# Layer 0's normalisation moved to the values' PSUM bank, and its and the convolution's elementwise instructions given places in the written order

## The chip, the cores and the metric

The kernel runs on one core of one Trainium2 chip. The metric is the device time of one execution in microseconds; the time of a kernel is the median of its runs. The core's engines are TensorE (PE, with its weight loads shown as PEld), VectorE (DVE), ScalarE (ACT), GpSimd (POOL) and SyncE (SP, which issues the DMAs). Each engine takes its instructions in the order of its own queue.

## The reference, cut to what matters

The reference is a two-layer diffusion backbone in fp32 over 2048 tokens plus 256 context tokens, 1024 channels. Each layer normalises, projects, mixes in two branches, projects out and adds. The change lies in the mixer of layer 0:

```python
def even_mixer(px, pc, lam_p, subln, conv_w, lam_init, row, col, need_ctx):
    ...
    o = lax.map(lambda qb: diff_attend(qb, k_all, v_all, lam), q_blocks)
    ...
    out_a = diff_attention_post(o, subln, lam_init).astype(px.dtype) * jax.nn.silu(ga)
    out_b = short_conv(bb, cb, ub, conv_w) * jax.nn.silu(gb)
```

`diff_attend` takes two softmaxes over 2304 keys for each of 8 heads and subtracts one, times lambda, from the other, before the product with the values. `diff_attention_post` is an RMS norm over the 64 channels of a head. `short_conv` multiplies two projections, c and u, runs a three-tap convolution along the tokens, and multiplies by a third projection, b.

## The kernel before, in words

Layer 0's attention is `attention0`. It works on pairs of 128-query tiles: 64 periods j, each with two tiles n, for 8 heads of 16 tiles. For a tile, with m one of the two softmaxes: QK writes scores of 768 keys into one of two PSUM buffers "ps" (each two banks, L981); TR, one VectorE instruction, copies the scores out and takes their minimum (`reduce_scores`, L758); EX is the exponential over 2304 keys on ScalarE (L1020); CF, CD, PS and PA combine the two softmaxes, the first CD=192 columns on VectorE (L1034) and the rest in two halves of 1056 columns on GpSimd (L1039, L1044); T transposes on TensorE (L1051), E copies the result out on ScalarE (L1058); AV is the product with the values (L1068) into "po", a pool with a single bank; MA and MD add the two halves of po into the tile "ob" (L1079, L1089).

The order is written out by hand in `ATT_ORDER`: a list of operations with a planned time in ns each. An operation of period j stands at its time plus j times `ATT_PERIOD` (17966). The operations of all periods are sorted by that time and issued in that order; the planned times set only the order. `pin` chains an instruction to the pinned one before it on the same engine, so that pinned instructions keep that order. Instructions that aren't pinned are placed in their queue by the framework's scheduler.

The convolution's three projections fill TensorE: `conv_units` yields 2592 matmuls in 108 groups of 24 (L704), all into one PSUM bank "y0". The ten F of a period issue 4.18 matmuls each (`FILL`), and an F stops at the end of a group. At a group's end elementwise instructions follow, none of them pinned: after the first projection ScalarE copies the bank out (L719), after the second VectorE multiplies it (L721), after the third come three taps (POOL L728, DVE L729, L730), the gate (DVE L735) and the last product (POOL L739).

At the end of every fourth tile pair of an odd head MD starts `normalise` for the tile ob of 512 tokens: `squares` on ScalarE (L769), `means` with four small products "pms" (L775) and six small VectorE and GpSimd instructions on "f" and "zf" (L779 to L784), `rows` with four transposing products "pf" (L789) and a copy "fr" (L792), `scale` with a product "pr" (L796; each of the nine shows as two matmuls), a load of the gate "ga" (L798) and two VectorE instructions (L799, L800). The four steps are issued 1000, 2500, 8000 and 13000 ns of planned time after MD. Only their matmuls are pinned. The three products take the scores' buffers: `fin` is a `_Bank` over the pool of ps. There are 16 normalisations, every other period of the odd heads.

When the convolution is done, F loads the output weights (`load_wout`; 16 splits on POOL and DVE, L1171 and L1172), the gate rows and the first output product, in steps put into a list "late" at planned times. They end before `out_ctx`, which begins at the last QK.

Of the kernel before, what the change touches and what calls it, by code (L numbers as in the profile page):

```python
# [9 lines left out]
F32 = mybir.dt.float32  # L10
F32R = mybir.dt.float32r
AF = mybir.ActivationFunctionType
# [32 lines left out]
LX0:6277 QK011:6323 EX00:7115 TR011:7204 QK012:7706 F2:8053 TR012:8243 QK100:8753 F3:9100 TR100:9290 F4:9582  # L45
QK101:10064 LS01:10326 EX01:10530 TR101:10601 QK102:10847 F5:11194 F6:11676 TR102:12056 QK110:12158 F7:12941
LS10:13142 RC0:13296 F8:13423 CF0:13504 QK111:13905 LX1:14124 EX10:14374 CD0:14683 PS00:14988 TR110:14988
TR111:16024 PA00:16266 QK112:16703 TR112:17240 F9:17486 PS01:18785 LS11:18875 EX11:19108 PA01:20063 T00:21324
RC1:21701 T01:21760 CF1:21909 E00:21960 CD1:22582 PS10:22887 E01:23652 T02:23854 PA10:24165 E02:24490
T03:24637 T04:26502 PS11:26684 E03:27492 PA11:27963 E04:28084 T10:28378 T11:30472 E10:30907 E11:31499  # L50
AV0:32314 AV1:33174 T12:34234 E12:34870 T13:35017 E13:35653 T14:36282 E14:36700 AV2:36942 AV3:37802 AV4:38662
MA:41240 MD:47571
# [58 lines left out]


class _Bank(_Tags):


    width = None

    def tile(self, shape, dtype, tag, **kw):
        x = super().tile([shape[0], self.width or shape[1]], dtype, tag, **kw)
        return x[:, :shape[1]]  # L120
# [32 lines left out]
class Backbone:  # L153
# [488 lines left out]
    def conv_units(self, es):  # L642

        nc = self.nc
# [43 lines left out]
        for si, (j, ci) in enumerate(steps):  # L688
# [4 lines left out]
            for br in range(3):  # L693
# [17 lines left out]
                zc = z[:, 2:2 + n]  # L711
                if br == 0:
                    if first:
                        nc.gpsimd.memset(z[:, 0:2], 0.0)
                    else:
                        nc.gpsimd.tensor_copy(z[:, 0:2], ez)
                    if last:
                        nc.gpsimd.memset(z[:, n + 2:n + 3], 0.0)
                    nc.scalar.activation(zc, ps, AF.Copy)  # L719
                elif br == 1:  # L720
                    nc.vector.tensor_tensor(zc, ps, zc, ALU.mult)  # L721
                else:
# [5 lines left out]
                    nc.gpsimd.tensor_scalar(yc, z[:, i0 + 1:i1 + 1], wc[1], None, ALU.mult)  # L728
                    nc.vector.scalar_tensor_tensor(yc, z[:, i0:i1], wc[0], yc, ALU.mult, ALU.add)  # L729
                    nc.vector.scalar_tensor_tensor(yc, z[:, i0 + 2:i1 + 2], wc[2], yc, ALU.mult, ALU.add)  # L730
                    g = cp.tile([P, n + 1], F32, tag="g", name="cg")
                    nc.sync.dma_start(g[:, 1:1 + n], self.gb[j * P:j * P + P, t0:t0 + n])
                    if not first:
                        nc.vector.tensor_copy(g[:, 0:1], eg)
                    nc.vector.tensor_tensor(g[:, 1:1 + n], ps, g[:, 1:1 + n], ALU.mult)  # L735
                    if not last:
                        nc.gpsimd.tensor_copy(ez, z[:, n:n + 2])
                        nc.vector.tensor_copy(eg, g[:, n:n + 1])
                    nc.gpsimd.tensor_tensor(yc, yc, g[:, i0:i1], ALU.mult)  # L739
                    rows = slice(j * P, j * P + P)  # L740
                    cols = slice(t0 - 1 + i0, t0 - 1 + i1)
                    nc.sync.dma_start(self.mixb[0][rows, cols], yc)

                yield False
# [16 lines left out]
    def normalise(self, ep, pp, hp, o, zi, t0, n, tags=("sq", "fr", "sq"), bank="fin"):  # L761
# [3 lines left out]
        f = ep.tile([P, 8], F32, tag="f", name="f")[:, :2 * nt]  # L765

        def squares():
            self.sq = ep.tile([P, n], F32, tag=tags[0], name="sq")
            nc.scalar.activation(self.sq, o, AF.Square)  # L769

        def means():
            sq = self.sq
            pms = pp.tile([P, 512], F32, tag=bank, name="pms")
            for j in range(nt):
                self.pin(nc.tensor.matmul(pms[:, 2 * j:2 * j + 2], sq[:, j * P:j * P + P], self.blk,  # L775
                                          start=True, stop=True))

            zf = ep.tile([P, 8], F32, tag="zf", name="zf")[:, :2 * nt]
            nc.vector.tensor_copy(zf, zi.rearrange("p t h m -> p (t h) m")[:, :, 0])  # L779
            nc.vector.tensor_tensor(f, pms[:, :2 * nt], zf, ALU.mult)  # L780
            nc.vector.tensor_tensor(f, f, zf, ALU.mult)
            nc.vector.tensor_scalar(f, f, EPS, None, ALU.add)
            nc.gpsimd.tensor_tensor(f, f, self.mhalf.to_broadcast([P, 2 * nt]), ALU.pow)
            nc.vector.tensor_tensor(f, f, zf, ALU.mult)  # L784

        def rows():
            pf = pp.tile([P, 512], F32, tag=bank, name="pf")
# [102 lines left out]
    def attention0(self, ws, xs, ys, ps_t, ps_o):  # L890
# [1088 lines left out]
```

## Time and profile before

| | us |
|---|---|
| median of 3 runs | 3417.8 (3413.26 to 3419.44) |
| the profiled execution, its own time | 3412.76 |
| span of the profiled execution | 3411.0 |
| PE busy | 3224.7 |
| DVE busy | 1818.6 |
| ACT busy | 1604.1 |
| POOL busy | 1460.4 |

The span is the time from the first instruction to the last; the execution's own time lies 1.8 us above it. Busy times are over the whole span, and the stages differ: projections before and after the attention keep PE alone busy, while in the attention of layer 0 four engines work side by side.

### The profile page before, as it was taken

What the parts mean: (1) busy time and instruction counts of PE and PEld (TensorE: products, weight loads), DVE (VectorE), ACT (ScalarE), POOL (GpSimd) and SP (SyncE); (2) the same over time, 40 slices, a digit from 0 to 9 for tenths busy, and PEclk for the clock granted to TensorE, in tenths of its full rate; (3) what the DMA queues carried; (4) which work ended last, traced back from release to release, by engine and by line L of the source; (5) the groups of instructions that cost most, each with busy time, mean ns of one, the idle gap of its engine ahead of it and who ended that gap; (6) DMA issues with size and microseconds to landing.
All of it is one profiled execution on the core that took longest, in us unless ns stands there. A gap on an engine that the chain in (4) does not pass through costs nothing.

```text
span 3411.0 us, 54003 instructions
## 1 busy us (share of the span) xinstructions
PE 3224.7 (95%) x20386; PEld 2611.9 (77%) x20386; DVE 1818.6 (53%) x4155; ACT 1604.1 (47%) x2521; POOL 1460.4 (43%) x1185
## 2 busy tenths in 40 slices
PE   7999999999899988998899889999999999989999
PEld 6877777777677766776777657898888887878887
DVE  4343322477787787778777765421121014656733
ACT  4311133477777776776677634331111123656401
POOL 3133200388678867886778754300021001433400
PEclk9999999999999999999999989999999999999999
DMA  7366643623242334242323225443223157954143
GB/s 251 127 209 219 209 124 105 192 77 123 87 128 97 104 106 124 82 131 93 116 72 120 76 68 167 173 152 111 96 93 105 68 159 197 227 147 133 51 148 117
DMA packets 305317, 442.08 MB, mean 130 GB/s; under 512 B 54837, under 2 KB 212001, under 8 KB 292258
## 3 DMA queue, kind: packets, MB, share of 16 engines
q1 hardware_dynamic: 305058, 438.64, 40.4%
q8 instruction: 161, 2.64, 0.3%
q14 instruction: 98, 0.80, 0.1%
HBM read 307.59 MB, written 131.43 MB: 129 GB/s over the span
## 4 chain that ended last, share of the span: by engine, by line
PE 77%; DVE 10%; issue 6%; ACT 2%; POOL 2%; DMA 2%; SPq 0%; DVEq 0%; POOLq 0%; ACTq 0%
PE mm L394 27%; PE cmm L704 7%; PE po L1068 7%; PE y L1196 6%; PE pt L1051 6%; PE ps L981 6%; PE mm L406 4%; DVE s L758 4%; PE po L1894 3%; PE ps L1843 3%; PE pt L1877 3%; PE mps L307 1%; PE pc L1684 1%; ACT s L1020 1%; DVE f L784 1%
## 5 line engine op out<-in xcount | busy, mean ns | idle before, releaser
L758 DVE CUSTOM_DVE_ANT_0 s<-ps,zero 128x768 f32<-128x768 f32 x768 | 721.0, 953 | 215.6 <-PE ps L981 205.0
L394 PE MATMUL mm<-hx,wh 128*128 128x512 f32 (+1 forms) x2784 | 830.9, 382 | 0.0
L1044 POOL TENSOR_TENSOR s<-s 128x1056 f32<-128x1056 f32 x256 | 628.3, 2454 | 16.9
L394 PEld LDWEIGHTS mm<-hx,wh 128*128 128x128 f32 x2784 | 505.6, 188 | 122.5 <-issue 18.0
L394 PE MATMUL mm<-hx,wl 128*128 128x512 f32 (+1 forms) x1392 | 528.5, 380 | 0.0
L1058 ACT ACTIVATE aT<-pt 128x512 f32<-128x512 f32 (+1 forms) x640 | 345.4, 552 | 247.6 <-PE pt L1051 245.4
L981 PE MATMUL ps<-kst,qst 128*128 128x512 f32 (+1 forms) x1536 | 427.6, 367 | 36.1 <-DVE mx L758 34.1
L704 PE MATMUL cmm<-cx,wh 128*128 128x256 f32 x1728 | 353.7, 291 | 71.2 <-ACT z L719 25.3
L1039 POOL TENSOR_SCALAR s<-s,cf 128x1056 f32<-128x1056 f32 x256 | 314.2, 1227 | 240.1 <-DVE cf L1029 62.9
L1051 PE MATMUL pt<-sm,s 128*128 128x128 f32 x2304 | 357.0, 278 | 1.4 <-ACT aT L1058 1.1
L704 PEld LDWEIGHTS cmm<-cx,wh 128*128 128x128 f32 x1728 | 274.9, 191 | 93.5 <-ACT z L719 30.1
L1051 PEld LDWEIGHTS pt<-sm,s 128*128 128x128 f32 x2304 | 267.7, 142 | 70.6 <-issue 50.9
L1020 ACT ACTIVATE s<-s,bias 128x2304 f32<-128x2304 f32 x128 | 283.7, 2217 | 45.7 <-DVE bias L1009 45.2
L394 PEld LDWEIGHTS mm<-hx,wl 128*128 128x128 f32 x1392 | 261.3, 188 | 53.4
L1068 PE MATMUL po<-aT,vt 128*64 128x256 f32 x2304 | 290.8, 396 | 0.0
L1020 ACT ACTIVATE s<-s,low 128x2304 f32<-128x2304 f32 x128 | 283.6, 2216 | 5.1
L981 PEld LDWEIGHTS ps<-kst,qst 128*128 128x128 f32 x1536 | 236.1, 192 | 65.2 <-DVE mx L758 54.1
L704 PE MATMUL cmm<-cx,wl 128*128 128x256 f32 x864 | 247.6, 287 | 0.0
L1068 PEld LDWEIGHTS po<-aT,vt 128*64 128x64 f32 x2304 | 157.0, 140 | 99.8 <-issue 37.8
L1855 POOL TENSOR_SCALAR s<-s,rz 128x832 f32<-128x832 f32 (+1 forms) x128 | 122.8, 959 | 201.2 <-DVE rz L1854 150.9
L1196 PE MATMUL y<-wh,mh 128*128 128x512 f32 x544 | 182.4, 414 | 1.6 <-DVE mh L1274 1.6
L1196 PE MATMUL y<-wh,mx 128*128 128x512 f32 x544 | 174.4, 399 | 0.5 <-DVE mx L1276 0.5
(266 smaller groups left out, 4687.5 us busy)
## 6 DMA issues: line engine op xcount, KB each, us to landing
cx<-hx SPq DMA_DIRECT2D x72, 1024.0 KB
hx<-hx SPq DMA_DIRECT2D x18, 1024.0 KB
kst<-k SPq DMA_DIRECT2D x192, 96.0 KB
k<-k SPq DMA_DIRECT2D x32, 576.0 KB
xt<-in_x_dram SPq DMA_DIRECT2D x32, 512.0 KB
wm<-in_w_mod_dram SPq DMA_DIRECT2D x64, 256.0 KB
qst<-q SPq DMA_DIRECT2D x256, 64.0 KB
ws<-in_w_in_even_dram SPq DMA_DIRECT2D x27, 512.0 KB
```

Source lines behind the costliest of these rows:

```text
L394: mm = self.nc.tensor.matmul(ps[:, :n], p[:, kc], y, start=first, stop=last)
L406: mm = self.nc.tensor.matmul(ps[:, :3 * P], q[kc][:, ts] if isinstance(q, list) else q[:, kc, ts], p[:, kc], start=first, stop=last)
L704: yield nc.tensor.matmul(ps, w[p][:, kc, :], x[q][:, kc, :], start=i == 0, stop=i == 23)
L758: return self.nc.vector.tensor_tensor_reduce(dst, ps, self.zero.to_broadcast([P, n]), -QS, BIGGEST, ALU.add, ALU.min, mx)
L981: pin(nc.tensor.matmul(ps[:, k0:k1], q[:, qc:qc + P], k[:, k0:k1], start=True, stop=True))
L1020: pin(nc.scalar.activation(it.s[m], it.s[m], AF.Exp, bias=bias, scale=-1.0, accum_out=it.Z[:, m:m + 1]))
L1039: pin(nc.gpsimd.tensor_scalar(x, x, it.cf, 1.0, ALU.mult, ALU.mult))
L1044: pin(nc.gpsimd.tensor_tensor(it.s[0][:, cs], it.s[0][:, cs], it.s[1][:, cs], ALU.add))
L1051: pin(nc.tensor.transpose(pt[:, i * P:i * P + P], it.s[0][:, k0:k0 + P], self.ident))
L1058: pin(nc.scalar.activation(it.aT[g][:, 0:k, n * P:n * P + P], it.pt.pop(g)[:, 0:k * P].rearrange("p (k q) -> p k q", q=P), AF.Copy))
L1068: pin(nc.tensor.matmul(it.po[c:c + 64, 0:256], vts[it.h][:, kt, :], it.aT[g][:, i, :], start=kt < 2, stop=kt >= 16, tile_position=(0, c)))
L1196: self.pin(self.nc.tensor.matmul(ps[hf] if isinstance(ps, list) else ps[:, cs], x, w[kc][:, cs], start=kc == 0 and i == 0, stop=kc == 7 an ...
```

## The change

The list of operations is a new one, with a longer period; CD grows from 192 to 256 columns. The class `_Bank` goes, and the normalisation takes its products in the bank po. Its four steps become nine, each at its own planned time, at most three of them in one period, and all their instructions but the DMAs are pinned. The last normalisation and those of the context keep the four steps (`quarters`). The convolution's elementwise instructions are pinned too, at planned times after the end of their group; after a group's end every F within 1500 ns of planned time issues nothing. ga is loaded into the buffer of fr instead of that of the squares. ob gets a sixth buffer. The steps after the convolution get new times.

```diff
-ATT_PERIOD = 17966
-Y0 = 14000
-FILL = 418
+ATT_PERIOD = 18602
+Y0 = 7000
+FILL = 430
+WGAP, YGAP = 1900, 3900
 ATT_ORDER = """
-QK000:0 QK001:565 TR000:1662 TR001:2697 QK002:4229 QK010:4576 F0:4923 TR002:4928 F1:5405 LS00:6014 TR010:6168
...
-AV0:32314 AV1:33174 T12:34234 E12:34870 T13:35017 E13:35653 T14:36282 E14:36700 AV2:36942 AV3:37802 AV4:38662
-MA:41240 MD:47571
+QK000:0 QK001:829 TR000:904 F0:1176 F1:1658 TR001:1939 QK002:2140 TR002:2975 LS00:4169 QK010:4502 QK011:5439
+LX0:6231 TR010:6660 TR011:7695 QK012:7972 EX00:8335 TR012:8731 QK100:8881 F2:9446 QK101:9928 F3:10275
+LS01:10517 TR100:10671 EX01:11337 TR101:11707 QK102:12342 F4:12689 TR102:12879 QK110:13607 RC0:13915 F5:13954
+LS10:14073 CF0:14227 LX1:14277 F6:14436 TR110:14447 QK111:14918 PS00:15584 F7:16137 CD0:16824 EX10:17085
+PS01:17230 TR111:17230 QK112:17555 F8:17902 TR112:18266 PA01:18470 F9:18949 LS11:19352 EX11:19556 PA00:20912
...
+T12:34303 E11:34503 E12:35095 T13:35721 T14:36986 AV0:39786 E13:40567 AV1:40646 E14:41159 AV2:44116 AV3:48056
+AV4:48916 MA:50951 MD:52686
 """
@@ conv_units
                 if br == 0:
...
-                    nc.scalar.activation(zc, ps, AF.Copy)
...
+                    yield [(400, lambda zc=zc, ps=ps: pin(nc.scalar.activation(zc, ps, AF.Copy))), (1500, edges)]
                 elif br == 1:
-                    nc.vector.tensor_tensor(zc, ps, zc, ALU.mult)
...
+                    yield [(400, lambda zc=zc, ps=ps: pin(nc.vector.tensor_tensor(zc, ps, zc, ALU.mult))),
+                           (1500, middle), (3000, lambda sides=sides: sides(0)), (4500, lambda sides=sides: sides(2)),
+                           (4600, edge)]
                 else:
...
+                    yield [(400, gate), (1500, out)]
@@ normalise
-        return squares, means, rows, scale
+        return squares, means, factors, scaled, rows, rows_out, spread, scale, gate
@@ attention0
-        CD = 192
+        CD = 256
...
-            fin = _Bank(ps_s, {"fin": "ps"})
-            fin.width = 1024
+            fin = _Tags(ps_o, {"fin": "po"})
...
-                    late.extend((now[0] + d, s) for d, s in zip((1000, 2500, 8000, 13000), steps))
+                        todo.extend((j + d // 100, t, st[i]) for i, (d, t) in enumerate((
+                            (0, 50), (0, 900), (0, 1300), (0, 6000), (100, 200), (100, 600), (200, 200), (200, 600),
+                            (200, 5000))))
+                for x in [x for x in todo if x[0] == j]:
+                    todo.remove(x)
+                    run_late(x[1], x[2])
...
             def F(j, f):
                 n_fill[0] += 1
+                if now[0] - ended[0] < 1500:
+                    return
...
                         if n_fill[1] % 24 == 0:
-                            next(fill)
+                            for d, step in next(fill):
+                                run_late(d, step)
+                            ended[0] = now[0]
                             break
...
-                        late.extend((now[0] + 12000 + 1050 * i, step) for i, step in enumerate(steps))
...
+                for i, step in enumerate(steps):
+                    run_late(6000 + WGAP * i, step)
```

`run_late(d, step)` puts a step into the list late at the present planned time plus d. The last hunk stands in a new function `after_conv`, itself put 6000 ns after the F that finds the convolution done.

## Rows read from the trace of the kernel before

**Rows 1.** Stretches: us, busy time (instructions) of PE, PEld, DVE, ACT, POOL; clock, DMA share, GB/s.

```profile
0.00:636.00 636.00, 618.23 (x3252) 484.72 (x3252) 211.00 (x494) 173.69 (x303) 131.15 (x131) 1.00 0.56 181
636.00:2030.60 1394.60, 1254.99 (x9106) 1009.68 (x9106) 1080.22 (x2615) 1002.45 (x1458) 1051.66 (x695) 0.98 0.32 103
2030.60:3411.00 1380.40, 1351.52 (x8028) 1117.47 (x8028) 527.40 (x1047) 427.91 (x760) 277.56 (x359) 0.99 0.43 133
```

**Rows 2.** PE's instructions by line, 636 to 1990 us: busy, mean ns, idle before, releasers.

```profile
L981 PE MATMUL ps<-kst,qst 128*128 128x512 f32 (+1 forms) x1536 | 427.6, 367 | 36.1 <-DVE mx L758 34.1 <-ACT g L629 0.7 <-DVE eg L738 0.6
L704 PE MATMUL cmm<-cx,wh 128*128 128x256 f32 x1728 | 353.7, 291 | 71.2 <-ACT z L719 25.3 <-DVE cg L735 18.0 <-DVE bias L1009 15.7
...
L775 PE MATMUL pms<-sm,sq 128*128 128x2 f32 x120 | 15.8, 254 | 6.9 <-DVE mx L758 6.9
L796 PE MATMUL pr<-fr,sm 2*128 2x512 f32 x28 | 15.6, 637 | 0.6 <-DVE mx L758 0.6
L789 PE MATMUL pf<-sm,f 128*2 128x128 f32 x112 | 15.4, 283 | 19.4 <-DVE mx L758 10.9 <-DVE zi L1025 5.8 <-DVE f L784 2.8
```

**Rows 3.** Fourteen stretches between two MD (L1089) with a normalisation: one, and the sum.

```profile
1334.63:1360.51 25.88, 22.99 (x158) 17.64 (x158) 19.89 (x46) 14.63 (x22) 18.20 (x13) 0.93 0.16 36
...
sum 361.38, PE 310.56 PEld 238.92 DVE 283.52 ACT 230.43 POOL 247.47; mean PE 22.18 PEld 17.07 DVE 20.25 ACT 16.46 POOL 17.68
```

**Rows 4.** The 46 other stretches between two MD, 684.5 to 1944.9 us: their sum.

```profile
sum 899.06, PE 834.27 PEld 689.71 DVE 702.46 ACT 702.45 POOL 719.92; mean PE 18.14 PEld 14.99 DVE 15.27 ACT 15.27 POOL 15.65
```

**Rows 5.** The 11 of these 46 in which PE idled under 0.3 us: their sum.

```profile
sum 194.54, PE 193.98 PEld 161.59 DVE 159.42 ACT 152.09 POOL 163.43; mean PE 17.63 PEld 14.69 DVE 14.49 ACT 13.83 POOL 14.86
```

**Rows 6.** Timeline at the end of a convolution group, 1116.9 to 1119.7 us.

```profile
1117.37 0.28 PE L704 MATMUL cmm<-cx,wl 128*128 128x256 f32 x1
...
1117.54 0.41 DVE L1089 TENSOR_TENSOR ob<-po,ft 64x256 f32<-64x256 f32 x1
1117.87 0.94 DVE L758 CUSTOM_DVE_ANT_0 s<-ps,zero 128x768 f32<-128x768 f32 x1
...
1118.74 0.41 DVE L721 TENSOR_TENSOR z<-cmm,z 128x256 f32<-128x256 f32 x1
...
1119.21 0.50 PE L704 MATMUL cmm<-cx,wh 128*128 128x256 f32 x2 [1.56 <-DVE bias L1009]
```

**Rows 7.** Timeline of a normalisation's first products, 860.3 to 865.0 us.

```profile
860.95 1.02 PE L775 MATMUL pms<-sm,sq 128*128 128x2 f32 x8 [1.00 <-DVE mx L758]
...
862.21 1.26 DVE L781 TENSOR_TENSOR f<-f,zf 128x8 f32<-128x8 f32 x1
...
863.50 1.09 DVE L782 TENSOR_SCALAR f<-f 128x8 f32<-128x8 f32 x1
```

**Rows 8.** DVE's and ACT's instructions by line and form, 636 to 1990 us.

```profile
L1020 ACT ACTIVATE s<-s,bias 128x2304 f32<-128x2304 f32 x127 | 281.5, 2217 | 45.7 <-DVE bias L1009 45.2
...
L1034 DVE SCALAR_TENSOR_TENSOR s<-s,cf 128x192 f32<-128x192 f32 x127 | 56.6, 446 | 3.7
...
L1020 ACT ACTIVATION_READ_ACCUMULATOR s<-s,bias 128x1 f32 x127 | 24.4, 192 | 0.0
...
L719 ACT ACTIVATE z<-cmm 128x256 f32<-128x256 f32 x36 | 13.7, 381 | 1.8 <-PE cmm L704 1.6
...
L799 DVE TENSOR_TENSOR ob<-ob,pr 128x512 f32<-128x512 f32 x14 | 9.6, 688 | 6.9 <-PE pr L796 6.9
...
L792 ACT ACTIVATE fr<-pf 2x512 f32<-2x512 f32 x14 | 8.1, 580 | 12.9 <-PE pf L789 12.8
...
L780 DVE TENSOR_TENSOR f<-pms,zf 128x8 f32<-128x8 f32 x15 | 2.4, 161 | 1.1 <-PE pms L775 1.0
```

**Rows 9.** SP's own waits over the span: line, what it waited for, us, times, longest.

```profile
SPq L673 <- PE cmm L704: 251.5, 25, 28.0
...
SPq L798 <- PE pms L775: 48.1, 10, 24.6
```

**Rows 10.** The instructions on tile f: duration ns min/median/max, first and last start, forms.

```profile
L784 DVE TENSOR_TENSOR f<-f,zf x20: 162/1474/2385, 484.9 to 2038.9; 128x8 f32<-128x8 f32 x16, 128x4 f32<-128x4 f32 x4
```

More of the change, by code (lines that the diff above doesn't have):

```diff
@@ L110, in tile @@
         return self.pool.tile(shape, dtype, tag=self.tags.get(tag, tag), **kw)
[L113 to L120, printed above, removed]
 class _Turns:
@@ L735, in conv_units @@
[L735 to L742, printed above, removed]
@@ L744, in conv_units, with middle, sides, edge @@
-                yield False
+                    def middle(z=z, yc=yc, wc=wc, i0=i0, i1=i1):
+                        pin(nc.gpsimd.tensor_scalar(yc, z[:, i0 + 1:i1 + 1], wc[1], None, ALU.mult))
+                    def sides(v, z=z, yc=yc, wc=wc, i0=i0, i1=i1):
+                        pin(nc.vector.scalar_tensor_tensor(yc, z[:, i0 + v:i1 + v], wc[v], yc, ALU.mult, ALU.add))
+                    def edge(z=z, last=last):
+                        if not last:
+                            pin(nc.gpsimd.tensor_copy(ez, z[:, n:n + 2]))
@@ new lines, in conv_units, with gate, out @@
+                    yield [(400, lambda zc=zc, ps=ps: pin(nc.vector.tensor_tensor(zc, ps, zc, ALU.mult))),
+                           (1500, middle), (3000, lambda sides=sides: sides(0)), (4500, lambda sides=sides: sides(2)),
+                           (4600, edge)]
+                else:
+                    def gate(ps=ps, g=g, first=first, last=last):
+                        if not first:
+                            pin(nc.vector.tensor_copy(g[:, 0:1], eg))
+                        pin(nc.vector.tensor_tensor(g[:, 1:1 + n], ps, g[:, 1:1 + n], ALU.mult))
+                        if not last:
+                            pin(nc.vector.tensor_copy(eg, g[:, n:n + 1]))
+                    def out(yc=yc, g=g, i0=i0, i1=i1, rows=slice(j * P, j * P + P),
+                            cols=slice(t0 - 1 + i0, t0 - 1 + i1)):
+                        pin(nc.gpsimd.tensor_tensor(yc, yc, g[:, i0:i1], ALU.mult))
+                        nc.sync.dma_start(self.mixb[0][rows, cols], yc)
+                    yield [(400, gate), (1500, out)]
@@ L759, in reduce_scores, with normalise @@
                                               ALU.min, mx)
-    def normalise(self, ep, pp, hp, o, zi, t0, n, tags=("sq", "fr", "sq"), bank="fin"):
+    def normalise(self, ep, pp, hp, o, zi, t0, n, tags=("sq", "fr", "fr"), bank="fin", order=False):
         nc = self.nc
@@ L943, in attention0, with run_late @@
             obs, zis = {}, {}
-            now, late, last = [0], [], []
+            now, late, last, todo = [0], [], [], []
+            def run_late(d, *steps):
+                late.extend((now[0] + d, s) for s in steps)
+                late.sort(key=lambda x: x[0])
             def tile_of(j, n):
@@ L994, in QK @@
                     ks2.close()
-                    fin.pool, fin.tags, fin.width = self.pool(ys, "fin", 1, space=PSUM), {}, None
+                    fin.pool, fin.tags = self.pool(ys, "fin", 1, space=PSUM), {}
                     y1 = self.pool(ys, "y1", 1, space=PSUM)
@@ L1111, in F, with after_conv @@
                         if n_fill[1] % 24 == 0:
[L1112 removed]
+                            for d, step in next(fill):
+                                run_late(d, step)
+                            ended[0] = now[0]
                             break
                         continue
[L1115 to L1123 removed]
+                    if not done:
+                        done.append(run_late(6000, after_conv))
+            done, ended = [], [-10000]
+            def after_conv():
+                cs.close()
+                fp, steps = self.load_wout(0, ws, xs)
+                rows = self.gate_rows(0, 1, _Tags(fp, {"grow": "ws"}, {"grow": 2}), ps_t, ep, "sq")
+                first = self.out_first(_Tags(ep, {"m0": "ob", "m1": "ob"}, {"m0": 6, "m1": 6}))
+                for i, step in enumerate(steps):
+                    run_late(6000 + WGAP * i, step)
+                for i in range(3):
+                    run_late(6000 + 16 * WGAP + 1000 * i, lambda: next(rows, None))
+                for i in range(9):
+                    run_late(Y0 + YGAP * i, lambda: next(first, None))
             OPS = {"QK": QK, "TR": TR, "LS": LS, "LX": LX, "EX": EX, "RC": RC, "CF": CF, "CD": CD_, "PS": PS, "PA": PA, "T": TP,
```

107 lines of the change are left out of this document (53 added, 54 removed).

## The prediction

> **What bounds the kernel now.** I first split the span into stretches [rows 1]. Layer 0's attention, from its first score product to its last MD, takes 1394.6 of 3411.0 us, and the diff touches nothing outside it but the last output steps. PE is busy for 1255.0 us of it. DVE, ACT and POOL are busy for 1080, 1002 and 1052 us, so none of the four is full. PE is the nearest to it, and the question is what PE waits for.
>
> PE's instructions by line answer that [rows 2]. The idle time ahead of the convolution's matmuls (L704) is 71.2 us, ahead of the scores (L981) 36.1 us, ahead of the normalisation's three products 6.9 + 19.4 + 0.6 = 26.9 us. Together that is 134 us.
>
> Then I cut the attention at its 64 MD, one to a period. Of the 60 stretches before the convolution ends, 14 hold a normalisation and take 361.38 / 14 = 25.81 us each [rows 3]. The other 46 take 899.06 / 46 = 19.54 us [rows 4]. Eleven of those have next to no PE idle time and take 194.54 / 11 = 17.69 us, all but 0.05 us of it PE busy [rows 5]. The planned period is 17.97 us. So the written order does what it was written for where nothing unwritten comes between: PE runs back to back. The excess sits in the stretches in which instructions without a place come in: 6.27 us more for a normalisation, 1.85 us more in the other stretches.
>
> Two timelines show how. At a group's end [rows 6] the last matmul of the group starts at 1117.37; DVE takes MD's addition and a score reduction first, and the product that empties the bank only at 1118.74. The next convolution matmul, which wants the same bank, starts at 1119.21 after 1.56 us of idle PE. At a normalisation [rows 7] the product pms waits 1.00 us for a score buffer, since it takes one of the two; DVE then spends 1.26 and 1.09 us on two 8-column instructions, in front of the score reductions that would free the other.
>
> **The change, part by part.**
>
> Normalisation. PE's own work on it stays: 15.8 + 15.4 + 15.6 us for 15 of them [rows 2], 3.12 us each. Of the 6.27 us, 6.27 - 3.12 = 3.15 us is wait, 14 x 3.15 = 44 us. Some of it is time at the lower clock level, as in the stretch shown with a mean granted clock of 0.93 [rows 3]; it goes or stays with the waits, and I count nothing beside them. The products leave the score buffers, and come after MD, when po is free until the next AV0: in the list from 52686 to 39786 + 18602 = 58388, 5.7 us. If PE still waits out each emptying of the bank in full, that is 0.16 + 0.58 + 0.69 = 1.43 us (L780, L792, L799) [rows 8], 20 us for the 14, and 24 us are gained; with none, 44. I take the middle, -34.
>
> Convolution. 71.2 us of idle time [rows 2] lie at 108 group ends. The new list spaces the F so that the one after a group's end comes at least 1.5 us later, and emptying the bank (0.38 us, L719 [rows 8]) has its place 0.4 us after. An exponential in the way costs 2.22 + 0.19 us on ACT [rows 8]; going through the ten F of the list, the next allowed F comes after that too in eight cases, and in two (the group ending at F5 or F8) about with it. I keep a quarter: -53. The ends are -71 (all gone) and -20 (the evacuations by DVE and ACT still come late, because fixed places order a queue and don't hold a time).
>
> Scores. The 36.1 us at L981 [rows 2] are PE waiting for a reduction, partly behind the normalisation and the convolution's taps. I take half, -18; the ends are 0 and -36.
>
> Longer pipeline. The first MD stands at 52.7 instead of 47.6 us in the list, so the last comes that much later: +5.
>
> CD. 128 instructions of 192 columns take 446 ns [rows 8]; 256 columns at most 446 x 256/192 = 595, so +0.15 x 128 = 19 us on DVE, and less on POOL. DVE is idle for 1394.6 - 1080.2 = 314 us of the stage [rows 1], which hides it: 0. If DVE becomes the bound, +19.
>
> After the convolution. FILL grows 3%, and the convolution is done at F 603 instead of 620, two periods earlier in the list; the output weights then come in over 36 us instead of 17. The convolution's matmuls are as many. I take 0 with ends of -15 and +15, a sixth of the tail from 1944.9 to 2030.6 us.
>
> DMAs. ga goes to fr's buffer and so waits on SP for the product pr instead of pms; behind it in SP's queue stand the loads of the convolution's inputs and of k and q. L798 waited 48.1 us before already, up to 24.6 us once, and the queue itself waits 251.5 us for convolution buffers (L673) [rows 9], so loads run ahead: 0. What it costs when that lead is gone is one late load, some us.
>
> Sum: -34 - 53 - 18 + 5 = -100 against the profiled execution's 3412.8, so 3312.8. The median of the runs shown, 3417.8, lies 5.0 above that execution, so I predict 3318. The list gives a cross-check: it spans 63 x 17.966 + 47.571 = 1179 us before and 63 x 18.602 + 52.686 = 1225 after. The stage took 1394.6, 215 above its list; the forecast leaves 1294.6, 70 above the new one.
>
> **The rivals.**
>
> All the waits go: -71 - 44 - 36 + 5 = -146, 3272. For it: the 11 quiet stretches [rows 5]. Against it: with 3.1 us of normalisation in every other period and the taps, the four queues have less slack than in those. Chance 0.12.
>
> The convolution's wait stays: the places are behind exponentials often enough that PE meets a full bank as before. Then -34 - 18 + 5 = -47, 3371. For it: the bank is still a single one. Against it: the 1.5 us without an F. Chance 0.13.
>
> DVE holds the normalisation back: -100 + 34 = -66, 3352. What speaks for it is L784, an 8-column product which takes between 162 and 2385 ns [rows 10], in DVE's queue ahead of reductions. Chance 0.13. The Trainium skill, page "SBUF — State Buffer", section "Who interferes with whom", says that a VectorE instruction with two SBUF inputs and a GpSimd instruction that reads SBUF exclude each other for the whole instruction. L784's spread agrees, and by that rule the sum would be this rival's, as a fixed place does not move GpSimd's long additions.
>
> One bank is too few, and the kernel is slower. Three products in 14 normalisations give 42 places where PE comes to po and stops until ACT or DVE has made the operand or emptied the bank, with the values' products queued behind. The normalisation's gain is then gone, and -53 - 18 + 5 = -66 is left, so it decides from 66 / 42 = 1.6 us a place. A full exponential with its read, 2.41 us, and a mean emptying of 0.48 us [rows 8] make 2.9 x 42 = 122: +56, 3474. Against it: the 5.7 us window and places at 15.5 us of the period, where the list has no exponential before 17.1. Chance 0.04. The Trainium skill, page "Perfetto Trace Analysis", section "Matmuls", speaks against the change here: independent groups should rotate through different PSUM banks so that emptying one overlaps the next. Rows 7 show products that rotate through two banks and still wait, so the trace does not bear it out for this pair.
>
> The change does nothing that counts: convolution and normalisation both wait as before, -18 + 5 = -13, 3405, and 3424 with CD's +19 on DVE. Chance 0.03.
>
> **How the numbers follow.** The forecast has 0.55. Cases below 3272 are half of the first rival; above 3385 lie the last two and little else. So 3268 to 3385 for 8 in 10. A measurement of this kernel can tell about 0.2%, 7 us, from no change. Faster: 0.55 + 0.12 + 0.13 + 0.13 and half of the last rival, 0.94. Same: 0.02. Slower: 0.04.
>
> **What would show it.** In the changed profile PE's idle time ahead of L704's successor should be about 18 us instead of 71, stretches with normalisation products should differ from the others by about 2 us or less for each of three periods, and the sum of 60 stretches should fall by about 100 us. Quiet stretches of about 18 us would show that the new list costs nothing; if all stretches lie at 18.6 or above, the list itself has become the bound. PE idle ahead of AV (L1068's successor) or of the three products above 66 us would be the slower rival. The forecast is wrong if DVE's idle time ends on PE no less often than before, or if the tail after the convolution takes over 15 us more.

## The result, and the profile after

The changed kernel takes 3460.9 us (median of 4 runs, 3453.8 to 3465.5) against 3415.8 for the kernel before beside it: a ratio of 1.0129, with an interval of 1.0109 to 1.015. It is slower by 45 us where 100 less were forecast. The profiled execution took 3461.8 us, its span 3459.9.

The stretches after, with the columns of [rows 1] (the middle one ends at the last MD):

```profile
0.00:640.00 640.00, 618.76 (x3257) 485.27 (x3257) 213.06 (x498) 174.40 (x304) 132.26 (x131) 1.00 0.56 180
640.00:2062.50 1422.50, 1306.79 (x9101) 1022.74 (x9101) 1096.42 (x2607) 986.40 (x1457) 1039.62 (x694) 0.96 0.31 98
2062.50:3459.90 1397.40, 1355.91 (x8030) 1120.87 (x8028) 530.47 (x1051) 428.47 (x760) 280.72 (x360) 0.99 0.44 134
```

The last MD comes 31.9 us later than before, and what follows it takes 17 us more. In the attention PE is busy for 1307 us instead of 1255, on as many instructions, and its granted clock is 0.96 instead of 0.98. Its lines, as in [rows 2]:

```profile
L1014 PE MATMUL ps<-kst,qst 128*128 128x512 f32 x1532 | 460.4, 383 | 81.5 <-DVE mx L766 75.2 <-DMA kst<-k 3.7 <-issue 1.3
L1084 PE MATMUL pt<-sm,s 128*128 128x128 f32 x2304 | 361.0, 281 | 18.8 <-POOL s L1077 12.7 <-ACT aT L1091 5.8
L697 PE MATMUL cmm<-cx,wh 128*128 128x256 f32 x1727 | 356.4, 291 | 4.4 <-DMA cx<-hx 2.0 <-DVE cg L743 1.5 <-ACT z L716 0.4
L1101 PE MATMUL po<-aT,vt 128*64 128x256 f32 x2304 | 303.4, 400 | 0.0
```

The convolution's wait is gone: 71.2 us before [rows 2], 4.4 here. The normalisation's three products fall from 26.9 us of idle time to 7.3. But the scores rise from 36.1 to 81.5, and the transposes (L1084) from 1.4 to 18.8. From the first score product to the last MD, PE's idle time over all lines falls only from 139 to 117 us, and PE's busy time grows by more than that, 53 us.

The stretches answer to [rows 3 to 5]. A normalisation is now spread over three periods, so 30 of the 60 stretches hold a product of one (first row, their sum), and 30 don't (second). The third is the sum of the ten of these with under 0.3 us of PE idle time:

```profile
sum 714.45, PE 635.43 PEld 487.78 DVE 563.52 ACT 472.92 POOL 504.64; mean PE 21.18 PEld 16.26 DVE 18.78 ACT 15.76 POOL 16.82
sum 593.06, PE 568.91 PEld 458.40 DVE 461.37 ACT 446.08 POOL 466.49; mean PE 18.96 PEld 15.28 DVE 15.38 ACT 14.87 POOL 15.55
sum 186.53, PE 185.74 PEld 151.51 DVE 147.78 ACT 149.57 POOL 154.06; mean PE 18.57 PEld 15.15 DVE 14.78 ACT 14.96 POOL 15.41
```

All 60 take 1307.5 us (1260.4 before). Those with a product of a normalisation take 23.8 us each, the others 19.8: 4.0 apart, where the prediction named 2 or less. The quiet ones take 186.53 / 10 = 18.65 us instead of 17.69. The prediction named 18.6 in all stretches as the sign that the list itself had become the bound; single quiet ones still lie between 17.6 and 19.9. PE is busy for all but 0.08 us of each, so in them it is PE's own time that has grown, by 0.94 us.

What the scores wait for is VectorE. In the timeline of one such place (start, duration, engine, line) the gate product of a normalisation, 2.86 us long, and a split of the convolution's weights, 2.56 us, stand ahead of the reduction that frees a score bank:

```profile
914.32 2.38 POOL L1077 TENSOR_TENSOR s<-s 128x1024 f32<-128x1024 f32 x1
914.38 2.86 DVE L819 SCALAR_TENSOR_TENSOR ob<-ga,sublnc,ob 128x512 f32<-128x512 f32 x1
916.73 2.72 POOL L1077 TENSOR_TENSOR s<-s 128x1024 f32<-128x1024 f32 x1
917.17 2.56 DVE L659 TENSOR_TENSOR wl<-ws,wh 128x256 fp32r<-128x256 f32 x1
919.66 0.94 DVE L766 CUSTOM_DVE_ANT_0 s<-ps,zero 128x768 f32<-128x768 f32 x1
920.67 0.79 PE L1014 MATMUL ps<-kst,qst 128*128 128x512 f32 x1 [3.65 <-DVE mx L766]
```

Each of the two ends 0.3 to 0.5 us after an addition of GpSimd ends. The same weight split takes 0.40 us at its shortest. The Trainium skill, page "SBUF — State Buffer", section "Who interferes with whom", says that a VectorE instruction with two SBUF inputs and a GpSimd instruction that reads SBUF shut each other out for a whole instruction; these rows agree.

Behind the last MD, PE waits 9.1 us for the first output rows. The last-but-one normalisation's store (L820) now comes 5 us after it, and the load of those rows (L1322) stands behind that store in SP's queue (before, that load was issued 21 us ahead of the last MD):

```profile
2066.34 0.75 DVE L819 SCALAR_TENSOR_TENSOR ob<-ga,sublnc,ob 128x512 f32<-128x512 f32 x1 [1.06 <-DMA ga<-ga]
2067.11 0.32 SPq L820 DMA_DIRECT2D mixa<-ob  x1
2067.53 0.39 SPq L1322 DMA_DIRECT2D mx<-mixa  x1
2072.18 1.22 PE L1246 MATMUL y<-wh,mh 128*128 128x512 f32 x2 [9.12 <-DVE mh L1324]
```

### The profile page after: what moved, and what is told of

Read it like the earlier page. It is cut to its first block, busy times and chain, and to the rows that moved or that the text cites. A ratio compares the mean times of both kernels' runs of the same rounds, so it can differ in the third digit from the quotient of the medians.

```text
span 3459.9 us, 54092 instructions
## 1 busy us (share of the span) xinstructions
PE 3281.5 (95%) x20386; PEld 2628.9 (76%) x20386; DVE 1839.9 (53%) x4155; ACT 1589.3 (46%) x2521; POOL 1452.6 (42%) x1185
## 5 line engine op out<-in xcount | busy, mean ns | idle before, releaser
L1077 POOL TENSOR_TENSOR s<-s 128x1024 f32<-128x1024 f32 x256 | 614.0, 2413 | 9.4
L1014 PE MATMUL ps<-kst,qst 128*128 128x512 f32 (+1 forms) x1536 | 461.4, 383 | 82.2 <-DVE mx L766 75.2
L1091 ACT ACTIVATE aT<-pt 128x512 f32<-128x512 f32 (+1 forms) x640 | 332.7, 550 | 197.6 <-PE pt L1084 193.2
L1072 POOL TENSOR_SCALAR s<-s,cf 128x1024 f32<-128x1024 f32 x256 | 309.2, 1218 | 261.6 <-ACT low L1048 108.1
L1084 PE MATMUL pt<-sm,s 128*128 128x128 f32 x2304 | 361.0, 281 | 18.8 <-POOL s L1077 12.7
L1084 PEld LDWEIGHTS pt<-sm,s 128*128 128x128 f32 x2304 | 273.8, 144 | 65.1 <-ACT aT L1091 18.6
L1101 PE MATMUL po<-aT,vt 128*64 128x256 f32 x2304 | 303.4, 400 | 0.0
L1246 PE MATMUL y<-wl,mh 128*128 128x512 f32 x544 | 174.3, 399 | 0.0
```

The source lines that it names most:

```text
L1014: pin(nc.tensor.matmul(ps[:, k0:k1], q[:, qc:qc + P], k[:, k0:k1], start=True, stop=True))
L1072: pin(nc.gpsimd.tensor_scalar(x, x, it.cf, 1.0, ALU.mult, ALU.mult))
L1077: pin(nc.gpsimd.tensor_tensor(it.s[0][:, cs], it.s[0][:, cs], it.s[1][:, cs], ALU.add))
L1084: pin(nc.tensor.transpose(pt[:, i * P:i * P + P], it.s[0][:, k0:k0 + P], self.ident))
L1091: pin(nc.scalar.activation(it.aT[g][:, 0:k, n * P:n * P + P], it.pt.pop(g)[:, 0:k * P].rearrange("p (k q) -> p k q", q=P), AF.Copy))
L1101: pin(nc.tensor.matmul(it.po[c:c + 64, 0:256], vts[it.h][:, kt, :], it.aT[g][:, i, :], start=kt < 2, stop=kt >= 16, tile_position=(0, c)))
```

## The experiments

My theory after these traces: the places are worth something, and the new list (order, FILL, CD) costs more than they give. The rival: the places themselves cost it, through VectorE. The ratios below are to runs of the kernel before taken beside each experiment; their medians lie between 3412.1 and 3416.3, so differences of medians between experiments carry up to 4 us of that.

**1. The list and the places, apart.** The kernel before with the new list, period, FILL and CD (and six ob buffers), its own bodies kept; and the changed kernel with the old list, FILL and CD.

```diff
# e1_list: before.py
-ATT_PERIOD = 17966; FILL = 418; CD = 192; old ATT_ORDER
+ATT_PERIOD = 18602; FILL = 430; CD = 256; new ATT_ORDER
# e2_places_old_list: after.py
-ATT_PERIOD = 18602; FILL = 430; CD = 256; new ATT_ORDER
+ATT_PERIOD = 17966; FILL = 418; CD = 192; old ATT_ORDER
-run_late(6000 + WGAP * i, step)
+run_late(6000 + 1050 * i, step)
...
```

> The kernel before with the new list of operations, its period, FILL 430 and CD 256 (and six ob buffers); normalisation in the score buffers, elementwise instructions without places, as before. Theory A (the new list itself is worse: more idle time ahead of the scores, longer VectorE instructions with CD 256): slower than before by 45 us or more, at least 3460, with the stretches that hold neither conv wait nor normalisation at 18.6 or more instead of 17.7. Theory B (the list is neutral, the fixed places and the single bank cost the time): within 10 us of before, 3406 to 3426.

> The changed kernel with the list of before (period 17966, FILL 418, CD 192, the steps after the convolution at about their old times). Theory A: the fixed places and the bank po bring what was forecast, 60 to 100 us, so 3316 to 3356. Theory B: slower than before, 3440 to 3470, as the changed kernel is.

The list alone: 3461.7, ratio 1.0145 (1.0129 to 1.016). The places alone: 3379.7, ratio 0.9903 (0.9888 to 0.9918). So on the old list the places are worth 33 us, a time between the two theories' ranges, and without the places the list costs 50, as theory A of its run said. The two don't add: -33 and +50 would give 3433, and the changed kernel takes 3460.9. On the new list the places are worth nothing that shows (3461.7 without them, 3460.9 with). With the list alone the convolution waits no less, as this part of its waits shows (line, what it waited for, us, times, longest):

```profile
PE cmm L706 <- ACT z L721: 34.3, 20, 4.0
PE cmm L706 <- DVE z L723: 24.0, 19, 3.1
PE cmm L706 <- DVE cg L737: 20.3, 14, 3.0
```

So the F that I read as spaced for the group's end give nothing until the emptying has its place too. In e2, with the old spacing, the convolution's wait is 10.0 us: the places alone do it, together with the rule that skips an F within 1.5 us of a group's end.

**2. The two halves of the places**, both with the old list, FILL and CD.

```diff
# e3: conv_units, F and run_late from after.py, normalise from before.py
# e4: normalise, fin and MD from after.py, conv_units and F from before.py
```

> The kernel before with only the convolution's instructions in fixed places and no F within 1500 ns of a group's end. Theory A: the 71 us of idle time ahead of the convolution's matmuls shrink to under 15 and most of that reaches the end: 3355 to 3385. Theory B (two-input VectorE instructions meet GpSimd's long additions in their fixed places and hold up the score reductions): 3410 to 3445, with idle time moved from the convolution's matmuls to the scores.

> The kernel before with only the normalisation in the bank po, in nine steps with fixed places over three periods (and six ob buffers). Theory A: a normalisation's extra falls from 6.3 to about 4 us in all: 3375 to 3395. Theory B: PE stops at po and the tail waits for the last normalisation, which now ends two periods later: 3420 to 3450.

The convolution's places alone: 3391.4, 0.994 (0.9923 to 0.9956). The normalisation's alone: 3411.4, 0.9992 (0.9982 to 1.0002). Both lie between the ranges of their two theories. In e3 57 us of wait ahead of the convolution go, and 20 us come off the time. PE now idles elsewhere: the scores' idle time rises to 43.7, the transposes' to 7.8, pms' to 20.1.

```profile
L1001 PE MATMUL ps<-kst,qst 128*128 128x512 f32 x1526 | 427.9, 369 | 43.7 <-DVE mx L774 41.5 <-PE pt L1071 0.7 <-DMA kst<-k 0.3
L1071 PE MATMUL pt<-sm,s 128*128 128x128 f32 x2294 | 358.2, 279 | 7.8 <-ACT aT L1078 7.1 <-POOL s L1064 0.3
L705 PE MATMUL cmm<-cx,wh 128*128 128x256 f32 x1722 | 345.5, 289 | 14.7 <-ACT z L724 6.5 <-DVE cg L751 5.0 <-DVE z L744 2.3
L791 PE MATMUL pms<-sm,sq 128*128 128x2 f32 x120 | 17.0, 264 | 20.1 <-DVE mx L774 16.5 <-ACT s L1040 2.8 <-ACT low L1035 0.7
```

In e4 the last MD comes 14.5 us earlier and the tail takes 13 us more: the late normalisation gives the gain back, its store 4.1 us behind the last MD and the load of the output rows behind it.

**3. CD, FILL and the tail, one by one.**

```diff
# f1: after.py            -CD = 256     +CD = 192
# f2: e2                  -CD = 192     +CD = 256
# f3: e2                  -FILL = 418   +FILL = 430
# f4: e2, the nine places of the normalisation (3, 2) alone
-(0, 6000), (100, 200), (100, 600), (200, 200), (200, 600), (200, 5000)
+(0, 6000), (0, 6200), (0, 6600), (0, 8500), (0, 8900), (0, 10500)
```

> The changed kernel with CD back at 192, all else as changed. Theory C (the wider VectorE part, 665 instead of 446 ns for each of 128 instructions, 28 us of VectorE time, is most of the list's loss): at least 25 us faster than the changed kernel, 3436 or below. Theory D (the order and spacing of the new list, whatever CD): within 12 us of the changed kernel, 3449 to 3473.

> Fixed places and bank po on the old list as in e2_places_old_list (3380), with CD 256. Theory C: 25 us or more slower than that, 3405 or above. Theory D: within 12 us, 3368 to 3392.

> As e2_places_old_list (3380) with FILL 430 instead of 418: 3 per cent more convolution matmuls in a period, the convolution done some two periods earlier. Theory D lets it be within 8 us, 3372 to 3388; if the fuller periods are what costs on the new list, 3395 or above.

> As e2_places_old_list (3380), with the nine steps of the last but one normalisation (head pair 3, tokens 1024 to 1535) placed within 10.5 us after its MD instead of over three periods. If the tail behind the last MD is 17 us longer there because that normalisation ends late and the loads of the output stage queue behind its store on SP, the tail goes back from 1397 to about 1381 and the time falls to 3360 to 3370. If something else makes the tail longer: 3375 to 3385.

f1: 3460.2, as with 256. f2: 3374.7, 5 less than e2. CD costs nothing with either list. f4: 3368.8, 0.9866 (0.9843 to 0.989): the load of the output rows is again issued 20 us ahead of the last MD, and the tail falls from 1397.0 to 1381.7 us, so its cause is shown. The surprise is f3: 3417.9, 38 us more than e2 from FILL alone. By stretches, 1 to 57 take 1186.6 us instead of 1154.9, and 58 to 63 take 145.4 instead of 143.9, though they hold 30 convolution matmuls instead of 101. The 71 matmuls moved forward are worth about 8 us at 119 ns from end to end; the first stretches pay 32 for them, and the last give nothing back. The stretch from the convolution's end to the last MD shows it, in f3 and in e2 (PE, PEld, DVE, ACT, POOL busy; clock):

```profile
1887.60:2015.90 128.30, 104.33 (x575) 70.72 (x573) 84.82 (x175) 69.03 (x106) 85.22 (x62) 0.87 0.18 58
```

```profile
1893.30:1981.80 88.50, 69.25 (x377) 47.91 (x375) 56.08 (x106) 40.77 (x65) 57.23 (x46) 0.88 0.23 78
```

It is 39.8 us longer, at about the same clock (0.87 and 0.88), and begins only 5.7 us earlier.

**4. Is it the collision behind the convolution, the number, or the order?** One stretch of f3, with the output weight's splits in it, took 42 us. So: f3 with these spread; FILL half way; the new list with FILL 418; and f4 with CD 256.

```diff
# g1: after.py   -FILL = 430   +FILL = 418     (output weight's steps timed as in e2)
# g2: f3         -run_late(6000 + 1050 * i, step)   +run_late(6000 + 1900 * i, step)   ... (the other late steps too)
# g3: f4         -CD = 192     +CD = 256
# g4: f4         -FILL = 418   +FILL = 424
```

> The changed kernel with FILL back at 418 (and the output weight's steps at their old times, since the convolution then ends 2.7 stretches later). Theory 'FILL': with the old list, FILL 430 alone cost 38 us (3379.7 to 3417.9), and it costs as much with the new list: about 3423. Rival 'the new order': the order of the list itself is what costs, and FILL counts only where the old list put the convolution's groups: 3450 to 3460. An even split gives 3440.

> Old list, all fixed places, CD 192, FILL 430, as in the run of 3417.9, but the output weight's steps spread as in the changed kernel (one in 1.9 us instead of 1.05, first output rows one in 3.9 us). Theory 'collision': the 42.3 us stretch after the convolution, 22 above the mean, is the output weight's splits meeting a normalisation; spread out it shrinks and about 20 us come back: 3395 to 3400. Rival 'fuller stretches': the loss is in stretches 1 to 57, which were 1 us each longer, and the steps only move: 3410 to 3420.

> Old list, all fixed places, the last-but-one normalisation early (3368.8 with CD 192), with CD 256. CD 256 alone gave 5 us with the old list (3379.7 to 3374.7): 3364 if it adds, 3369 if that was chance. If the longer causal-difference instruction on VectorE did cost something that the tail hid, 3375 or more.

> As the kernel of 3368.8 (old list, all places, last-but-one normalisation early, CD 192), with FILL 424, half way to 430. If what FILL costs grows evenly (a fuller stretch is a longer one), 3385 to 3390. If it is a matter of where the groups' ends fall against the normalisations (a phase), it need not lie between: about 3369 or 3405 and more.

g2: 3413.8, so the collision is at most 4 of the 38. g4: 3402.3, 33 more than with 418 for half the step, so the cost is not in proportion either. g3: 3364.1, 0.9854 (0.9839 to 0.9869), the best of all. g1: 3435.0, 1.006 (1.0048 to 1.0073). With the places on, FILL is 26 of the list's cost, and the order itself, against e2's 3379.7, is 55. Now e2 and g1 differ in the order (with its period) and in CD, which costs nothing. PE's lines in each, e2 first, ahead of them the whole attention (columns of [rows 1]):

```profile
635.20:1981.80 1346.60, 1255.76 (x9106) 1011.76 (x9106) 1066.10 (x2611) 1000.38 (x1457) 1057.45 (x694) 0.97 0.32 105
L1012 PE MATMUL ps<-kst,qst 128*128 128x512 f32 x1528 | 431.8, 371 | 50.7 <-DVE mx L764 48.4 <-PE pt L1082 1.0 <-DMA kst<-k 0.4
L1099 PE MATMUL po<-aT,vt 128*64 128x256 f32 x2304 | 281.6, 389 | 0.4 <-ACT aT L1089 0.4
```

```profile
635.60:2037.70 1402.10, 1296.48 (x9106) 1015.19 (x9106) 1073.86 (x2611) 988.39 (x1457) 1037.59 (x694) 0.97 0.31 101
L1014 PE MATMUL ps<-kst,qst 128*128 128x512 f32 x1532 | 456.3, 380 | 68.1 <-DVE mx L766 64.9 <-issue 0.9 <-DVE cg L742 0.5
L1101 PE MATMUL po<-aT,vt 128*64 128x256 f32 x2304 | 298.9, 395 | 0.0
```

The same instructions keep PE busy for 24.5 and 17.3 us more. Over the whole attention PE is busy for 41 us more (1255.8 to 1296.5), on as many instructions, and idle for 15 more (91 to 106). Together that is the 55. The busy part comes from changes of kind. Where PE doesn't idle and the clock is full, a score matmul ends 430 ns after a matmul with the values, but 236 to 248 after a transpose or a matmul of the convolution; the first of a run with the values ends 360 ns after whatever went before, the next ones 100; a transpose ends 260 ns after a matmul with the values and 109 after another transpose. The new list has three runs with the values in a period (AV0 and AV1; AV2; AV3 and AV4), the old two. Counted from the first MD to the 61st, the runs go from 120 to 180, the score products right behind values from 0 to 180, and the transposes right behind values from 120 to 0. An estimate from these: 180 x 0.19 + 60 x 0.26 - 120 x 0.15 = 32 of the 41 us. Both lists were there to be counted before any run; the price of a score behind values was not, since the kernel before has none.

**5. Two attempts on that.** One run of values less; and the taps put off to where the list has no addition of GpSimd's (as VectorE's waits suggested), with the new list, with FILL 424 and on the best kernel.

```diff
# h1: after.py   -AV2:44116 AV3:48056   +AV2:48040 AV3:48056
# h2: after.py, h3: g4, h4: g3
-run_late(d, step)
+at = now[0] + d
+if d in (3000, 4500): at = tapped[0] = free_at(at)     # 0.5 us before to 2.4 behind a PA: later
+run_late(at - now[0], step)
...
```

> The changed kernel with one entry of the list moved: the third product with the values goes right ahead of the fourth, so that a stretch has two runs of values' products instead of three. Theory 'switches': a run's beginning costs PE 360 ns instead of 100 for its first matmul, and scores right behind values 430 instead of about 120 to 250; one run less saves 0.4 to 0.5 us in each of 60 stretches, 24 to 30 us: about 3434. Rival 'the order's other waits' (idle of PE before scores and transposes): unchanged, 3455 to 3465.

> The changed kernel with the convolution's two tap instructions on VectorE put off to the next stretch of the list in which GpSimd has no addition. Theory 'meeting': a tap that meets an addition takes 1.5 to 2.8 us instead of 0.48; the taps' mean falls from 1014 ns to 500 to 600, 30 us of VectorE's time, and with the idle time and the low clock behind it the time falls by 20 to 35 us: 3425 to 3440. Rival 'only VectorE's own time': VectorE has 2 us to spare in a stretch, the taps get shorter and the time stays: 3455 to 3465.

> The same edit on the kernel of 3402.3 (old list, all places, last-but-one normalisation early, FILL 424). Theory 'meeting': what FILL 424 cost against 418 (33 us) goes back for the most part: 3370 to 3385. Rival 'fuller stretches': 3395 to 3405.

> The same edit on the best kernel so far (3364.1: old list, all places, last-but-one normalisation early, CD 256, FILL 418), whose taps take 889 ns on average. Theory 'meeting': 28 us of VectorE's time less, 10 to 20 us of the whole: 3344 to 3354. Rival: 3360 to 3368.

h1: 3460.3, unchanged. Its rows say why:

```profile
L1014 PE MATMUL ps<-kst,qst 128*128 128x512 f32 x1532 | 460.2, 383 | 98.0 <-DVE mx L766 92.7 <-DMA kst<-k 2.6 <-issue 1.3
L1101 PE MATMUL po<-aT,vt 128*64 128x256 f32 x2304 | 286.6, 394 | 0.0
```

The values take 16.8 us less of PE, and the scores idle 16.5 us longer. This part of PE's extra time was real, but it lay beside a wait for VectorE.

h2: 3441.6, 19 less. h3: 3393.1, 9 less, between its two ranges. h4: 3378.6, 14 more, slower than either of its theories allowed. The taps did get shorter each time, in the median from 792 to 486, from 770 to 485 and from 492 to 484 ns (the rows: duration in ns, shortest, median, longest; the changed kernel, then h2):

```profile
L730 DVE SCALAR_TENSOR_TENSOR y<-z,vT,y x72: 457/792/2629, 660.5 to 1926.3; 128x256 f32<-128x256 f32 x56, 128x255 f32<-128x255 f32 x8, 128x257 f32<-128x257 f32 x8
```

```profile
L730 DVE SCALAR_TENSOR_TENSOR y<-z,vT,y x72: 466/486/2629, 657.0 to 1912.1; 128x256 f32<-128x256 f32 x56, 128x255 f32<-128x255 f32 x8, 128x257 f32<-128x257 f32 x8
```

So putting the taps off gains something in two of three kernels, but the sign is not steady. That a tap put off then stands in front of something else is a guess; what the traces show of it stands in the last section.

**6. All remedies on the new list, and the gate.**

```diff
# k1: g1 with h1's, h2's and f4's edits
# k2: g3    -(200, 5000)   +(200, 3600)
```

> The new list with everything that helped elsewhere: FILL 418 (-26), taps put off (-20 with FILL 430), two runs of values' products (-1), the last-but-one normalisation early (-11 to -13). If the gains add: 3461 - 58 = 3403. If the new order has a cost of its own that none of these touches, it stays 30 to 50 above the same kernel with the old list (3378.6 with CD 256): 3405 to 3430. If the order's cost was only these things: 3375 to 3385.

> The kernel of 3364.1 (old list, all places, last-but-one normalisation early, CD 256) with the normalisation's gate instruction 1.4 us earlier in its stretch, where the list has no addition of GpSimd's. Theory 'meeting': the gate falls from 1459 ns to 700 to 1000, 15 of them, and the time by 0 to 10 us: 3354 to 3364. Rival: its gate row's load has then not landed and VectorE waits: 3370 or more.

k1: 3446.9, 12 more than g1 although its tail is 17 us shorter (1378.4), and above every case that I had expected: the remedies don't add on this list. k2: 3366.7, as g3; the gate's mean stays at 1.5 us, most gates of the attention still overlap an instruction of GpSimd's in the trace, and VectorE now waits 7.9 us for the gate rows' load, as the rival supposed. Nothing that I did to the new list brings it near the old one.

Where does the idle part of the order's cost sit? Counting the score matmuls of the trace, two to a product and twelve products to a period, gives PE's idle time for each product. There are two score banks, so a product needs the reduction of the last but one to have ended, and that takes 953 + 81 = 1034 ns (the rows below, the changed kernel), as the list plans it. The slack is the product's place less that planned end.

```profile
L766 DVE CUSTOM_DVE_ANT_0 s<-ps,zero 128x768 f32<-128x768 f32 x766 | 715.9, 953 | 233.8 <-PE ps L1014 231.3 <-POOL s L1072 0.8
...
L766 DVE DVE_READ_ACCUMULATOR2_ANT mx<- 128x1 f32 x766 | 62.4, 81 | 0.0
```

| product | slack in the old list, us | PE idle, before | slack in the new list | PE idle, after | g1 |
|---|---|---|---|---|---|
| QK000 | 0.91 | 0.2 | 0.34 | 14.9 | 13.7 |
| QK001 | 0.26 | 5.6 | 0.13 | 12.9 | 3.8 |
| QK002 | 1.53 | 2.5 | 0.20 | 23.3 | 27.8 |
| the nine others | 0.36 to 0.84 | 27.1 | 0.15 to 2.07 | 30.4 | 23.0 |

Nearly the whole rise sits at the first three products of a period. The new list starts QK002 at 2140, 0.2 us behind the planned end of TR000 (904 + 1035 = 1939); the old one left 1.5 us there. That the slack is the cause is argued from the place of the waits, not shown: no kernel was run with these three products alone moved. Against it speaks that QK100 and QK101, with 0.15 and 0.16 us, wait little, and e1 above all, which has the same list and so the same slacks without the places. There the three products idle 4.6, 13.4 and 6.5 us, and all the scores together less than before, at a cost of 50 us:

```profile
L983 PE MATMUL ps<-kst,qst 128*128 128x512 f32 x1532 | 455.3, 379 | 32.5 <-DVE mx L760 31.2 <-DVE f L782 0.8 <-DMA kst<-k 0.2
```

From 8 us before, the three products go to 24 with the list alone and to 51 with the places too. So the slack alone does not make that wait, and the list costs as much without it.

## Why the prediction was wrong

By the medians, from 3415.8: the places with the old list, -36 (e2; 33 against the runs beside it); the new order with CD, +55 (g1 against e2); FILL, +26 (the changed kernel against g1). These close to +45 by construction, and they are one way of splitting it: with the list first, it is +50 for the list (e1) and -1 for the places on it.

The profiled executions split it by what PE does, from the first score product to the last MD. The clock record gives the time at the lower of the two levels (1.2 and 2.4 GHz): 65 us before, 116 after. A matmul takes about 1.8 times as long there (in the changed kernel, from end to end, 119 ns become 213 within the convolution, 233 become 426 for a score behind a transpose, 360 become 619 for the first of a run with the values), so 0.45 of PE's busy time at that level is counted as lost to it. What is left is PE's own work. These are estimates from one execution each, in us:

| kernel | length | PE idle | lost to the lower level | PE's own work |
|---|---|---|---|---|
| before | 1394 | 139 | 27 | 1228 |
| the changed kernel | 1425 | 117 | 44 | 1264 |
| e1, list alone | 1446 | 136 | 48 | 1262 |
| e2, places alone | 1347 | 91 | 26 | 1230 |
| g1, new order, FILL 418 | 1402 | 106 | 32 | 1265 |
| f4, old order, FILL 418 | 1355 | 93 | 31 | 1231 |
| g4, old order, FILL 424 | 1386 | 108 | 43 | 1235 |

Between before and after, idle time gives 22 us, the lower level takes 17, PE's own work 36, and the tail 17: +48, of the 49 by which the two executions differ. The forecast took 105 us of waits off (34, 53 and 18) and held the rest at nothing but +5.

**The step that failed first is "Longer pipeline", +5.** It was the only term that I gave the new order, for the later first MD, and that came as said (691.5 instead of 684.5). But I took the quiet stretches of the old list [rows 5] as the level that the new one would reach, and wrote off its planned period, 18.60 against 17.97 us, as if only the waits counted. The quiet stretches then took 18.65. The cross-check did not catch it: it let the stage's excess over its list fall from 215 to 70 us without asking what else the new order does. With the places on, the order was worth +55: 34 of PE's own work, mostly the changes of kind that can be counted in the diff, 15 of idle time and 6 of the lower level. With the list alone, 34 and 22 and no more idle time (e1).

**The clock** is a part of that step. I wrote that its time "goes or stays with the waits" and counted nothing. The waits fell by 22 us, and the time at the lower level rose by 51.

**The second is "After the convolution", 0 with ends of -15 and +15.** FILL was 26 to 38 us, and the tail took 17 us more, past the 15 that I had named as a sign of being wrong. The earlier end is worth nothing, because the stretches without convolution are not shorter, and a fuller stretch costs more than its matmuls. By the table this is hardly PE's own work (g1 to the changed kernel: none; f4 to g4: 4 us) but idle time (12 and 15) and the lower level (12 and 12). Every run's mean granted clock over the span agrees: 0.982 to 0.986 in g1 against 0.976 to 0.980 in the changed kernel, 0.985 to 0.987 in f4 against 0.980 to 0.982 in g4. Why a little more convolution in a stretch does that, and as much for half the step, is not settled.

**Scores**: the sign was wrong. I took 18 of 36 us off; they rose to 50.7 with the old list (e2) and 81.5 with the new. In e3 the waits removed ahead of the convolution came back in part ahead of the scores, the transposes and pms.

**Convolution**: the mechanism was right, and more idle time went than forecast (71 to 4, not 18). As time it was 20 us with the old list (e3), against 53.

**Normalisation**: 27 us of idle ahead of the products became 7; as time it was 3 us (e4, whose interval takes in no change at all), against 34. 14.5 us were gained in the attention and 13 given back in the tail. I had read SP's queue for loads that run ahead; that the last-but-one normalisation now ends after the last MD, with its store in front of the loads of the output stage, I did not follow. f4 shows it.

**CD**, 0, was right (f1, f2), though its instructions took 665 ns and not at most 595. Of the **DMAs**, 0, the late loads at the head switches cost 3.7 us in the changed profile, as bounded.

**The slower rival**, one bank too few, is not what happened: PE waits 7 us ahead of the three products and none ahead of the values. "DVE holds the normalisation back" had the meeting of VectorE and GpSimd right and its place only in part: of the 8-column instructions one (L797, 1.26 us on average) still meets an addition, but the long ones now are the gate (1.9 us on average), the taps and the weight splits.

## What to carry to other kernels

A hand-placed order is a part of the change like any other: before crediting what its fixed places remove, go through the new order and the old and count how often PE changes from one kind of product to another, with the price of each change from the trace; here that gives 32 us. Then write down, for each product, how long after the planned release of its buffer it stands. Do not take a wait's time off twice: on a chain whose engines are all 70 to 90% busy, 57 us of wait removed ahead of one line came back as 20 of time. And follow the last instance of a loop that is spread over later periods into the stage behind it.

The old order with the new places, the last-but-one normalisation kept together and CD 256 takes 3364.1 us, 1.5% less than the kernel before and 2.8% less than the changed one.

## What I had not expected

Putting two VectorE instructions of half a microsecond up to 3 us later, in one third of the group ends, moved the time of 3.4 ms by 19 us down in one order and by 14 us up in another. Within the attention, most of these two changes is the clock. By the trace's clock record the changed kernel's attention holds 116 us at the lower level (1.2 GHz) and h2's 82, with 117 us of PE idle time in both; the best kernel's holds 65 and h4's 92, with 88 and 93 us of idle time. In h3 it is the idle time: 108 us in g4 and 94 in h3, with 102 and 109 us at the lower level. So the time at the lower level does not follow the sum of PE's idle time: the kernel before has more of that than the changed one (139 to 117) and less time at the lower level (65 to 116). What decides when the level falls is not shown here.
